# A one-level Strassen scheme for the down projection of a decoder block on one Trainium2 core

## The chip, the cores and the metric

The kernel runs on one core of one Trainium2 chip. The metric is the device time of one execution in microseconds. Before the change the median of three runs is 1080.75 us (1080.3 to 1080.9). The engines are TensorE (PE, with its weight loads as PEld), VectorE (DVE), ScalarE (ACT), GpSimd (POOL) and SyncE (SP), and sixteen DMA engines move data.

## The reference

One decoder layer on 512 tokens of width 1024. What matters here is the second half, the gated MLP with a short causal convolution, and the layer norm behind it:

```python
def channel_mixer(h, w_up, ffn_dw_w, ffn_dw_b, w_down):
    u = jnp.einsum("bsd,df->bsf", h, w_up)
    u = causal_depthwise_conv(u, ffn_dw_w, ffn_dw_b)
    val, gate = jnp.split(u, 2, axis=-1)
    return jnp.einsum("bsf,fd->bsd", val * jax.nn.silu(gate), w_down)

# in reference():
f = channel_mixer(h, w_up[l], ffn_dw_w[l], ffn_dw_b[l], w_down[l])
x = layer_norm(DEEPNORM_ALPHA * x + gate2 * f, ln2_g[l], ln2_b[l])
```

`w_down` is 2816 x 1024 in float32. The down projection is so a product of (512 x 2816) with (2816 x 1024).

## The kernel before

Float32 matmuls are made of three terms: an operand is split into a high part `h` (a ScalarE copy to the matmul's type) and a low part `l` (a VectorE subtraction), and a product is the sum of h.h, l.h and h.l. So each 128-row block of each product costs three matmuls, and each weight a split on ScalarE and VectorE.

The weights come through one stream (class `Stream`): SyncE loads an entry of up to 1 MB into one of two `stage` buffers, L126; a piece of up to 1024 columns is then split into one of three `wh` and `wl` buffers, L140 and L141. `get` returns the next piece and splits up to two ahead.

The stages, with their place in the profiled execution: the start-up (to about 50 us) normalizes the input, computes modulation vectors (`dot`, L326, on VectorE, from weights `wa` that `load_first` asks SyncE for, three buffers) and does the first projections; the head stage (to about 450 us) goes through eight heads, with a 31-tap convolution on VectorE (L460) beside TensorE's projections; gates, output projections and the first layer norm follow (to about 715 us), the up projection (to about 946 us), and the down projection with the last layer norm.

The work is written as a program in which each engine has one queue in order. The tile framework puts each engine's instructions in an order of its own, from their dependences, free buffers and priorities (`later(n)` lowers a priority by n places), and adds the semaphores.

GpSimd does little: it clears the padding of the convolution inputs (L454) and raises variances to the power -1/2 (`rstd_of`, L228), for the norm of the input, once for each head, and for each layer norm.

The up projection makes two units of 24 matmuls for each of the 22 blocks of the hidden layer. `up_pair(j, ...)` applies the convolution and the gate and splits the result into `acts[j]`, an `(ah, al)` pair of 128 features x 512 tokens.

The down projection (L1044 to L1084) runs in two passes. The first goes over the 22 blocks k and over four token tiles s of 128; its result is 512 columns (`pd0`) and then 256 columns (`pd1`). The last 256 columns have weights of their own (`wdq`), loaded and split during the first pass (`load_wq`, `split_wq`). The second pass does them token tile by token tile, so that the sum and the layer norm of one tile (`resid`, L865 and L866; `norm_rows`, L871 and L872) run beside the matmuls of the next. The stationary operand is a slice of `acts`, the moving one the weights.

Of the kernel before, what the change touches and what calls it, by code (L numbers as in the profile page):

```python
# [9 lines left out]
F32 = mybir.dt.float32  # L10
F32R = mybir.dt.float32r
# [13 lines left out]
CK = 31  # L25
DFF = 2816
NF = DFF // P
FK = 3
EPS = 1e-5
ALPHA = 2.0 ** 0.25  # L30
# [71 lines left out]
class Stream:  # L102
# [18 lines left out]
    def load(self, i):  # L121
        if i < len(self.entries) and i not in self.stage:
            ap, widths, pre = self.entries[i]
            w = sum(widths)
            t = self.pool.tile([P, 2048], F32, tag="stage", bufs=2, name=f"stage{i}")
            self.nc.sync.dma_start(t[:, :w], ap)  # L126
            self.stage[i] = t

    def prefetch(self, n):
# [43 lines left out]
def block_kernel(ctx: ExitStack, tc: tile.TileContext, a, out):  # L173
# [43 lines left out]
    def big(name):  # L217
        return [base.tile([P, ND, S], F32R, tag=f"big{i}", bufs=1, name=f"{name}{i}") for i in range(2)]
# [50 lines left out]
    for j in range(NF // 2):  # L269
        entries.append((a["wdn"][j], [768, 768]))  # L270
    st = Stream(nc, base, entries, 2)


# [327 lines left out]
    def drive(g):  # L601
        if g is not None:
            next(g, None)

    g = None
# [353 lines left out]
    drive(tr_[3])  # L959


    acts = []

    def up_out(p_, t):
        u = lg("u")
        act(u, p_, AF.Identity, bias=vc("fb", t), scale=vc("fw", t * FK + 2))
        stt(u[:, 1:], p_[:, :S - 1], vc("fw", t * FK + 1), u[:, 1:], ALU.mult, ALU.add)
        stt(u[:, 2:], p_[:, :S - 2], vc("fw", t * FK), u[:, 2:], ALU.mult, ALU.add)
        return u

    def up_pair(j, pv, pgt):
        r = [up_out(pv, j), up_out(pgt, NF + j)]
        act(r[1], r[1], AF.Silu)
        tt(r[0], r[0], r[1], ALU.mult)
        al = lg if j < 9 else xg if j < 13 else pg
        x, y = al("ah", F32R), al("al", F32R)
        split_to(x, y, r[0])
        acts.append((x, y))

    def half_unit(p_, w, half):  # L980
        c = slice(half * 256, (half + 1) * 256)
# [34 lines left out]
        up_pair(j, pv, pgt)  # L1016


    wqh, wql = big("wq")
    wq = []  # L1020

    NQ = NF // 2
    WQD = 3
    for c in range(NQ):
        if c < 8:
            x, y = wqh[:, c], wql[:, c]
        else:
            x, y = pg("wqh", F32R), pg("wql", F32R)
        wq.append((x, y))

    wqs = {}

    def load_wq(c):

        wqs[c] = lg("wqs")
        nc.sync.dma_start(wqs[c], a["wdq"][:, c * 512:(c + 1) * 512])

    def split_wq(c):
        t = wqs.pop(c)
        split_to(wq[c][0], wq[c][1], t)  # L1040

    pd0 = [ps("d0") for _ in range(NS)]
    pd1 = [ps("d1", (P, 2, DV)) for _ in range(2)]
    for k in range(NF):  # L1044
        wh, wl = st.get()
        if 1 <= k <= NQ:
            load_wq(k - 1)
        if WQD < k <= WQD + NQ:
            split_wq(k - WQD - 1)
        for s in range(NS):  # L1050
            sl = slice(s * P, (s + 1) * P)
            x, y = acts[k]
            f, l = (k == 0), (k == NF - 1)
            d1 = pd1[s // 2][:, s % 2]
            f1 = f and s % 2 == 0
            mm(pd0[s], x[:, sl], wh[:, 0:512], start=f, stop=False)  # L1056
            mm(pd0[s], y[:, sl], wh[:, 0:512], start=False, stop=False)  # L1057
            mm(pd0[s], x[:, sl], wl[:, 0:512], start=False, stop=l)  # L1058
            mm(d1, x[:, sl], wh[:, 512:768], start=f1, stop=False, skip_group_check=True)  # L1059
            mm(d1, y[:, sl], wh[:, 512:768], start=False, stop=False, skip_group_check=True)  # L1060
            mm(d1, x[:, sl], wl[:, 512:768], start=False, stop=l, skip_group_check=True)  # L1061
    lnr = []
    for name, tag in (("ln2_g", "wh"), ("ln2_b", "wl")):
        t = base.tile([P, D], F32, tag=tag, bufs=3, name=name)
        nc.sync.dma_start(t, a[name].broadcast_to([P, D]))
        lnr.append([t[:, 0:512], t[:, 512:1024]])
    ln2g, ln2b = lnr

    for s in range(NS):
        resid(xs[s][0], pd0[s], rows["gate2"][0])  # L1070
        resid(xs[s][1], pd1[s // 2][:, s % 2], rows["gate2"][1], slice(0, 256))
    for s in range(NS):
        sl = slice(s * P, (s + 1) * P)
        p_ = ps("d2", (P, DV))
        for k in range(NF):
            x, y = acts[k]
            wh, wl = wq[k // 2]
            w = slice((k % 2) * DV, (k % 2 + 1) * DV)
            mm(p_, x[:, sl], wh[:, w], start=(k == 0), stop=False)  # L1079
            mm(p_, y[:, sl], wh[:, w], start=False, stop=False)  # L1080
            mm(p_, x[:, sl], wl[:, w], start=False, stop=(k == NF - 1))  # L1081
        resid(xs[s][1], p_, rows["gate2"][1], slice(256, 512))
        norm_rows(xs[s], [xs[s][0], xs[s][1][:, :256], xs[s][1][:, 256:]], ln2g, ln2b,
                  lambda j: nc.sync.dma_start(out[s * P:(s + 1) * P, j * 512:(j + 1) * 512], xs[s][j]))  # L1084


# [95 lines left out]
```

## Time and profile before

| what | value |
|---|---|
| median of 3 runs | 1080.75 us |
| the profiled execution, its own time | 1080.97 us |
| its span, first to last instruction | 1079.2 us |
| TensorE busy | 1054.4 us, 98% |
| VectorE busy | 785.8 us, 73% |
| ScalarE busy | 456.6 us, 42% |
| GpSimd busy | 26.3 us, 2% |
| moved by DMA | 131.54 MB, mean 122 GB/s |
| granted TensorE clock, mean | 0.999 |

A busy TensorE is not TensorE at its peak, since matmuls are pipelined; what a stage costs is read from the starts of its matmuls and from the gaps between them. DMA-issuing instructions are not counted as busy.

### The profile page before, as it was taken

Reading aid. Unit: us, or ns where it says so; the run is one execution under the profiler, and the core shown is the slowest. Engines: PE = TensorE matmul, PEld = TensorE weight load, DVE = VectorE, ACT = ScalarE, POOL = GpSimd, SP = SyncE. Lnnn points to the kernel's source line nnn. Section 1 sums busy time; section 2 is a strip of 40 time slices with the busy share of each in tenths; the row PEclk is TensorE's granted clock in tenths of the full one; section 3 lists DMA queues with packets and bytes.
Section 4 is the critical chain, followed back from the end, with each engine's and each line's share of the span. In section 5 each row is a group of like instructions: output and inputs, shape, how many; then the busy total and the mean of one; then the engine's idle time right before and its main releaser. Section 6 shows DMA issues by size and latency. Waiting matters only on the chain. (4 is left out here: it accounts for less than half of the span.)

```text
span 1079.2 us, 14096 instructions
## 1 busy us (share of the span) xinstructions
PE 1054.4 (98%) x5648; PEld 906.9 (84%) x5648; DVE 785.8 (73%) x1252; ACT 456.6 (42%) x655; POOL 26.3 (2%) x41
## 2 busy tenths in 40 slices
PE   4999999999999999999999999999999999999997
PEld 2788898989898988887888889898888888888896
DVE  7989999979797979498984446957666565652264
ACT  5753544353444344551363333465444444442100
POOL 1000000000000000000000000110000000000001
PEclk9999999999999999999999999999999999999999
DMA  8822313222322222378642256022222323153112
GB/s 314 309 87 87 122 50 120 86 90 84 121 81 92 84 78 79 137 250 293 241 176 94 104 189 215 1 79 78 105 90 85 111 83 113 62 192 112 65 40 79
DMA packets 29316, 131.54 MB, mean 122 GB/s; under 512 B 3393, under 2 KB 5697, under 8 KB 19522
## 3 DMA queue, kind: packets, MB, share of 16 engines
q1 hardware_dynamic: 29250, 130.64, 34.1%
q8 instruction: 44, 0.72, 0.3%
q14 instruction: 22, 0.18, 0.1%
HBM read 128.53 MB, written 2.10 MB: 121 GB/s over the span
## 5 line engine op out<-in xcount | busy, mean ns | idle before, releaser
L141 DVE TENSOR_TENSOR wl<-stage,wh 128x1024 fp32r<-128x1024 f32 (+1 forms) x163 | 193.2, 1185 | 151.0 <-ACT wh L140 53.2
L140 ACT ACTIVATE wh<-stage 128x1024 fp32r<-128x1024 f32 (+1 forms) x163 | 168.0, 1030 | 291.7 <-PE up L442 58.0
L460 DVE SCALAR_TENSOR_TENSOR conv<-ci,vec,conv 128x512 f32<-128x512 f32 x240 | 178.8, 745 | 2.3
L441 PE MATMUL up<-h,wh 128*128 128x512 f32 x304 | 118.3, 389 | 0.0
L442 PE MATMUL up<-h,wh 128*128 128x512 f32 x304 | 118.3, 389 | 0.0
L444 PE MATMUL up<-h,wl 128*128 128x512 f32 x304 | 75.1, 389 | 0.0
L490 PE MATMUL v<-wl,h 128*128 128x256 f32 x256 | 72.5, 283 | 0.4 <-DVE wl L141 0.4
L489 PE MATMUL v<-wh,h 128*128 128x256 f32 x256 | 72.4, 283 | 0.0
L488 PE MATMUL v<-wh,h 128*128 128x256 f32 x256 | 72.4, 283 | 0.0
L441 PEld LDWEIGHTS up<-h,wh 128*128 128x128 f32 x304 | 57.1, 188 | 11.8
L444 PEld LDWEIGHTS up<-h,wl 128*128 128x128 f32 x304 | 57.1, 188 | 11.8
L442 PEld LDWEIGHTS up<-h,wh 128*128 128x128 f32 x304 | 57.1, 188 | 11.8
L782 PE MATMUL yb<-rh,wh 128*128 128x512 f32 x128 | 51.0, 398 | 0.0
L783 PE MATMUL yb<-rl,wh 128*128 128x512 f32 x128 | 50.5, 395 | 0.0
L784 PE MATMUL yb<-rh,wl 128*128 128x512 f32 x128 | 50.5, 395 | 0.0
L441 PE MATMUL gate<-h,wh 128*128 128x512 f32 x128 | 50.2, 392 | 0.0
L442 PE MATMUL gate<-h,wh 128*128 128x512 f32 x128 | 50.0, 390 | 0.0
L490 PEld LDWEIGHTS v<-wl,h 128*128 128x128 f32 x256 | 49.1, 192 | 0.6 <-DVE wl L141 0.6
L488 PEld LDWEIGHTS v<-wh,h 128*128 128x128 f32 x256 | 49.1, 192 | 0.0
L489 PEld LDWEIGHTS v<-wh,h 128*128 128x128 f32 x256 | 49.1, 192 | 0.0
L442 PE MATMUL g<-h,wh 128*128 128x512 f32 x112 | 43.7, 390 | 0.0
L441 PE MATMUL g<-h,wh 128*128 128x512 f32 x112 | 43.6, 389 | 0.0
(295 smaller groups left out, 2499.9 us busy)
## 6 DMA issues: line engine op xcount, KB each, us to landing
stage<-in_wstep SPq DMA_DIRECT2D x29, 1024.0 KB, 4.8
stage<-in_wup SPq DMA_DIRECT2D x22, 1024.0 KB, 4.8
wb<-in_wada SPq DMA_DIRECT2D x32, 512.0 KB, 5.3
stage<-in_wdn SPq DMA_DIRECT2D x11, 768.0 KB, 4.3
stage<-in_wret SPq DMA_DIRECT2D x8, 1024.0 KB, 5.9
stage<-in_wga SPq DMA_DIRECT2D x8, 1024.0 KB, 4.9
wa<-in_wada SPq DMA_DIRECT2D x14, 512.0 KB, 6.4
stage<-in_wgb SPq DMA_DIRECT2D x4, 1024.0 KB, 4.8
```

The source lines that it names most:

```text
L140: nc.scalar.activation(wh[:, :w], src, AF.Copy)
L141: nc.vector.tensor_tensor(wl[:, :w], src, wh[:, :w].bitcast(F32), ALU.subtract)
L441: mm(dst, wh[:, k * P:(k + 1) * P], hs[k][0], start=(k == 0), stop=False)
L442: mm(dst, wh[:, k * P:(k + 1) * P], hs[k][1], start=False, stop=False)
L444: mm(dst, wl[:, k * P:(k + 1) * P], hs[k][0], start=False, stop=(k == n - 1))
L460: stt(o, ci[:, t:t + S], vc("cw", i * CK + t), o, ALU.mult, ALU.add)
L488: mm(d, h_h[:, k, sl], wh[:, r], start=(k == 0), stop=False)
L489: mm(d, h_l[:, k, sl], wh[:, r], start=False, stop=False)
L490: mm(d, h_h[:, k, sl], wl[:, r], start=False, stop=(k == ND - 1))
L782: mm(p_, wh[:, w], rs_[k][0], start=(k == 0), stop=False)
L783: mm(p_, wh[:, w], rs_[k][1], start=False, stop=False)
L784: mm(p_, wl[:, w], rs_[k][0], start=False, stop=(k == 15))
```

## The change

The down projection is cut into halves in three ways: tokens 0 to 255 and 256 to 511; the 22 hidden blocks into even and odd ones (11 pairs); the output columns into 0 to 511 and 512 to 1023. Of the four weight blocks B11, B12, B21, B22 (each 1408 x 512) four sums are made: T1 = B11 + B12, T3 = B12 + B22, T2 = T1 + B22, T4 = T2 + B21. They lie in DRAM. Each is copied there by DMAs that GpSimd issues and then added to by DMAs with `accum_op`; 36 issues, of which the program names five at the top of each head's loop.

Seven products of 256 tokens x 1408 x 512 take the place of the two passes. They come in the order B11, T1, B21, T2, T3, B22, T4, each with 11 blocks x 2 token tiles x 3 terms. The activations stay unsplit in `F` (`u` of `up_pair`); their sums and differences are made on VectorE in place, and `split_op` splits the 256-token operand of a product, in `up_pair` for the first two products and for the others (`make`) during the product before. The weight stream has 21 entries of up to 1 MB here where it had 11 of 768 KB; entries of B12 and B22 are two DMAs with rows of 1 KB, as half of their columns lie in `wdq`. The results are gathered in `ca`, `c5`, `cb_`, `cc_` and in `xs`, with part of that work under `later(40)`. Token tiles 0 and 1 are finished after the sixth product, 2 and 3 after the seventh, whose last five blocks are done token tile by token tile. The rows of the last norm are loaded early, into the space of `h2`.

```diff
+    dram = ctx.enter_context(tc.tile_pool(name="dram", bufs=1, space=bass.MemoryType.DRAM))
+    for name in ("T1", "T2", "T3", "T4"):
+        wd[name] = dram.tile([P, NK, 512], F32, tag=name, name=name)
+    PIECES = ((0, 4), (4, 8), (8, 11))
...
+    for name in ("B11", "T1", "B21", "T2", "T3", "B22", "T4"):
+        for x, y in PIECES:
+            w = (y - x) * 512
+            entries.append((wblock(name, x, y), [1024, w - 1024]))
...
+    def sum_steps():
+        for dst, first, add in (("T1", "B11", "B12"), ("T3", "B12", "B22"), ("T2", "T1", "B22"), ("T4", "T2", "B21")):
+            for x, y in PIECES:
+                for f, src in wblock(first, x, y):
+                    nc.gpsimd.dma_start(wd[dst][:, x:y, f], src)
+                    yield
+            for x, y in PIECES:
+                for f, src in wblock(add, x, y):
+                    nc.gpsimd.dma_start(wd[dst][:, x:y, f], src, accum_op=ALU.add)
+                    yield
...
     for i in range(NH):
+        for _ in range(5):
+            drive(sums)
...
+        F.append(u)
+        if j % 2:
+            i = j // 2
+            x, y = F[2 * i], F[2 * i + 1]
+            ops1.append(split_op(i, x[:, 0:256]))
+            e = pg("e1", F32, (P, 256))
+            tt(e, x[:, 256:], y[:, 256:], ALU.subtract)
+            ops5.append(split_op(i, e))
+            tt(x[:, 256:], x[:, 256:], x[:, 0:256], ALU.subtract)
+            tt(x[:, 0:256], x[:, 0:256], e, ALU.subtract)
...
+    for n, R in enumerate((R1, R2, R1, R2, R3, R2, R3)):
+        new = n in (0, 1, 4)
+        ops = operands.pop(n)
+        made = []
+        for q in range(6 if n < 6 else 3):
+            w = st.get()
+            for kk in range(2 if q < 5 else 1):
+                k = 2 * q + kk
+                for t in range(2):
+                    sub_mm(R, ops[k], w, kk, t, new and k == 0, k == NK - 1)
+                if 1 <= n < 6:
+                    made.append(make(n + 1, k))
...
+        elif n == 4:
+            for t in range(2):
+                tt(cc_[t], R3[t], cb_[t], ALU.add)
+            with later(40):
+                for t in range(2):
+                    tt(c5[t], c5[t], cb_[t], ALU.subtract)
+                    tt(c5[t], c5[t], g2[0], ALU.mult)
+                    stt(xs[2 + t][0], xs[2 + t][0], ALPHA, c5[t], ALU.mult, ALU.add)
+                    tt(cc_[t], cc_[t], g2[1], ALU.mult)
+                    stt(xs[2 + t][1], xs[2 + t][1], ALPHA, cc_[t], ALU.mult, ALU.add)
+        elif n == 5:
+            for t in range(2):
+                tt(ca[t], R2[t], ca[t], ALU.subtract)
+            with later(40):
+                for t in range(2):
+                    tt(ca[t], ca[t], g2[1], ALU.mult)
+                    stt(xs[t][1], xs[t][1], ALPHA, ca[t], ALU.mult, ALU.add)
+                    finish(t)
         else:
+            ws_ = [st.get(ahead=2 - q) for q in range(3)]
+            for t in range(2):
+                for q in range(3, 6):
+                    for kk in range(2 if q < 5 else 1):
+                        k = 2 * q + kk
+                        sub_mm(R, ops[k], ws_[q - 3], kk, t, False, k == NK - 1)
+                tt(R[t], R[t], g2[0], ALU.mult)
+                tt(xs[2 + t][0], xs[2 + t][0], R[t], ALU.subtract)
+                finish(2 + t)
```

`sub_mm` issues the three matmuls of one block and token tile, 512 columns each; `make(n, k)` is one `split_op` on 256 columns, and for n = 2 a subtraction on 256 columns more; `finish(s)` is `norm_rows` and the two stores.

## Rows read from the trace of the kernel before

**Rows 1.** Busy time of each engine over the span, instructions.
```profile
PE 1054.4 (98%) x5648; PEld 906.9 (84%) x5648; DVE 785.8 (73%) x1252; ACT 456.6 (42%) x655; POOL 26.3 (2%) x41
```
**Rows 2.** Windows: stretch, length, busy of each engine, PE clock, DMA share, GB/s.
```profile
15.00:20.00 5.00, 0.95 (x2) 0.36 (x2) 4.05 (x12) 4.73 (x8) 1.75 (x2) 1.00 1.04 415
...
25.00:50.00 25.00, 24.00 (x117) 19.37 (x116) 24.41 (x49) 16.79 (x29) 0.00 (x0) 1.00 0.92 340
...
100.00:200.00 100.00, 100.00 (x580) 88.28 (x579) 97.89 (x158) 44.90 (x64) 2.81 (x5) 1.00 0.29 102
...
946.50:1039.50 93.00, 93.00 (x529) 81.06 (x529) 32.35 (x41) 24.21 (x33) 0.00 (x0) 1.00 0.33 110
1039.50:1071.20 31.70, 31.70 (x267) 31.54 (x265) 21.10 (x46) 0.00 (x0) 2.69 (x3) 1.00 0.14 51
```
**Rows 3.** Order of time on PE: start, duration, line, tiles; triples, stage's ends.
```profile
479.74 0.39 PE L782 MATMUL yb<-rh,wh 128*128 128x512 f32 x1
...
481.83 0.40 PE L782 MATMUL yb<-rh,wh 128*128 128x512 f32 x1
...
946.78 0.40 PE L1056 MATMUL d<-wh,ah 128*128 128x512 f32 x1
...
1069.77 0.28 PE L1080 MATMUL d<-wqh,al 128*128 128x256 f32 x1
...
1070.97 0.28 PE L1081 MATMUL d<-wql,ah 128*128 128x256 f32 x1
```
**Rows 4.** Order of time on DVE at the end of the kernel.
```profile
1071.29 0.43 DVE L865 TENSOR_TENSOR d<-d,grow 128x256 f32<-128x256 f32 x1 [3.39 <-PE d L1081]
...
1073.01 1.40 DVE L871 SCALAR_TENSOR_TENSOR xr<-xr,mv,ln_g 128x512 f32<-128x512 f32 x2
1074.33 1.41 DVE L872 SCALAR_TENSOR_TENSOR xr<-xr,rstd,ln_b 128x512 f32<-128x512 f32 x2
```
**Rows 5.** Groups by form on DVE and ACT: busy us, mean ns, idle before.
```profile
L141 DVE TENSOR_TENSOR wl<-stage,wh 128x1024 fp32r<-128x1024 f32 x141 | 172.1, 1221 | 102.2 <-PE up L444 41.8 <-PE gate L444 25.6 <-PE cg L444 14.6
L249 DVE TENSOR_TENSOR Rl<-R,Rh 128x256 fp32r<-128x256 f32 x8 | 3.3, 417 | 0.0
L865 DVE TENSOR_TENSOR d<-d,grow 128x512 f32<-128x512 f32 x4 | 2.8, 692 | 7.4 <-PE d L1058 7.4
...
L140 ACT ACTIVATE wh<-stage 128x1024 fp32r<-128x1024 f32 x141 | 149.4, 1060 | 240.7 <-PE up L442 51.9 <-PE v L489 41.7 <-PE yb L783 35.8
L248 ACT ACTIVATE Rh<-R 128x256 fp32r<-128x256 f32 x8 | 3.1, 384 | 0.2
```
**Rows 6.** Order of time on POOL: padding, a root of the input's norm, head 0's root.
```profile
0.73 0.23 POOL L454 MEMSET ci<- 128x30 f32 x3 [0.29 <-POOLq L1170]
...
10.06 0.57 POOL L228 TENSOR_TENSOR rstd<-ve,cst 128x1 f32<-128x1 f32 x1 [4.09 <-DVE ve L239]
...
115.28 1.42 POOL L228 TENSOR_TENSOR rstd<-hve,cst 128x4 f32<-128x4 f32 x1 [8.12 <-DVE hve L583]
```
**Rows 7.** Order of time: a VectorE operation that reads a mask, and SP's next load.
```profile
89.45 0.55 DVE L534 TENSOR_TENSOR scf<-sc,dm 128x384 f32<-128x384 f32 x1
...
90.03 0.33 SPq L504 DMA_DIRECT2D dm<-in_dmask  x1
```
**Rows 8.** DMA queue (packets, MB, share of sixteen engines); issues (KB, us to landing).
```profile
q1 hardware_dynamic: 29250, 130.64, 34.1%
...
stage<-in_wup SPq DMA_DIRECT2D x22, 1024.0 KB, 4.8
```
**Rows 9.** Modulation weights: a load's issue, its use on DVE, landing times of all.
```profile
33.80 0.33 SPq L314 DMA_DIRECT2D wa<-in_wada  x1
...
43.30 1.22 DVE L326 SCALAR_TENSOR_TENSOR junk<-wa,cb 128x1024 f32<-128x1024 f32 x1
...
DMA to landing us min/median/max: 3.8/6.5/10.3
```
**Rows 10.** Order of time on PE: the transposes of head 0's normed values.
```profile
122.02 1.03 PE L594 MATMUL rT<-cst,rn 128*128 128x128 f32 x8
```

More of the change, by code (lines that the diff above doesn't have):

```diff
@@ L27 @@
 NF = DFF // P
+NK = NF // 2
 FK = 3
@@ L125, in load @@
             t = self.pool.tile([P, 2048], F32, tag="stage", bufs=2, name=f"stage{i}")
-            self.nc.sync.dma_start(t[:, :w], ap)
+            if isinstance(ap, list):
+                v = t[:, :w].rearrange("p (j f) -> p j f", f=512)
+                for f, x in ap:
+                    self.nc.sync.dma_start(v[:, :, f], x)
+            else:
+                self.nc.sync.dma_start(t[:, :w], ap)
             self.stage[i] = t
@@ L268, in block_kernel, with wblock @@
         entries.append((a["wup"][j], [1024, 1024]))
-    for j in range(NF // 2):
-        entries.append((a["wdn"][j], [768, 768]))
+    dram = ctx.enter_context(tc.tile_pool(name="dram", bufs=1, space=bass.MemoryType.DRAM))
+    wd = {}
+    for name in ("T1", "T2", "T3", "T4"):
+        wd[name] = dram.tile([P, NK, 512], F32, tag=name, name=name)
+    PIECES = ((0, 4), (4, 8), (8, 11))
+    def wblock(name, x, y):
+        if name in wd:
+            return [(slice(0, 512), wd[name][:, x:y])]
+        r, c = int(name[1]) - 1, int(name[2]) - 1
+        n = a["wdn"][x:y].rearrange("j p (t f) -> p j t f", t=2)[:, :, r]
+        if c == 0:
+            return [(slice(0, 512), n[:, :, 0:512])]
+        q = a["wdq"].rearrange("p (j t f) -> p j t f", t=2, f=256)[:, x:y, r]
+        return [(slice(0, 256), n[:, :, 512:768]), (slice(256, 512), q)]
+    for name in ("B11", "T1", "B21", "T2", "T3", "B22", "T4"):
+        for x, y in PIECES:
+            w = (y - x) * 512
+            entries.append((wblock(name, x, y), [1024, w - 1024]))
     st = Stream(nc, base, entries, 2)
@@ L603, in drive @@
             next(g, None)
+    def sum_steps():
[8 more added lines that the diff above has]
+                    yield
+    sums = sum_steps()
     g = None
     for i in range(NH):
+        for _ in range(5):
+            drive(sums)
         if i == 0:
@@ L969, in up_out, with op_page, split_op @@
         return u
-    def up_pair(j, pv, pgt):
[L972 to L978, printed above, removed]
+    F = []
+    ops1, ops5 = [], []
+    def op_page(i):
+        return (pg if i < 8 else xg)("op", F32R, (P, 2, 256))
+    def split_op(i, src, neg=False):
+        o = op_page(i)
+        if neg:
+            act(o[:, 0], src, AF.Copy, scale=-1.0)
+            stt(o[:, 1], src, -1.0, o[:, 0].bitcast(F32), ALU.mult, ALU.subtract)
+        else:
+            split_to(o[:, 0], o[:, 1], src)
+        return o
+    def up_pair(j, pv, pgt):
+        u = up_out(pv, j, lg if j < 21 else pg)
+        r = up_out(pgt, NF + j, pg)
+        act(r, r, AF.Silu)
+        tt(u, u, r, ALU.mult)
+        F.append(u)
[8 more added lines that the diff above has]
+            tt(x[:, 0:256], x[:, 0:256], e, ALU.subtract)
     def half_unit(p_, w, half):
@@ L1042, in block_kernel @@
[L1042 to L1084, printed above, removed]
+    dt0 = base.tile([P, ND, S], F32, tag="big0", bufs=1, name="dtmp")
@@ new lines, in block_kernel, with finish @@
+    dt1 = base.tile([P, ND, S], F32, tag="big1", bufs=1, name="drow")
+    ca, c5, cb_, cc_ = [[dt0[:, 2 * n + t] for t in range(2)] for n in range(4)]
+    lnr = []
+    for n, name in enumerate(("ln2_g", "ln2_b")):
+        r = [dt1[:, 2 * n + h] for h in range(2)]
+        for h in range(2):
+            nc.sync.dma_start(r[h], a[name][:, h * 512:(h + 1) * 512].broadcast_to([P, 512]))
+        lnr.append(r)
+    ln2g, ln2b = lnr
+    g2 = rows["gate2"]
+    def finish(s):
+        norm_rows(xs[s], [xs[s][1], xs[s][0]], ln2g, ln2b,
+                  lambda j: nc.sync.dma_start(out[s * P:(s + 1) * P, j * 512:(j + 1) * 512], xs[s][j]))
@@ new lines, in block_kernel, with make, sub_mm @@
+    R1, R2, R3 = [[ps(f"d{n}") for _ in range(2)] for n in range(3)]
+    def make(n, i):
+        x, y = F[2 * i], F[2 * i + 1]
+        if n == 2:
+            o = split_op(i, y[:, 0:256])
+            tt(y[:, 0:256], y[:, 0:256], x[:, 0:256], ALU.subtract)
+            return o
+        src = {3: x[:, 0:256], 4: x[:, 256:], 5: y[:, 0:256], 6: y[:, 256:]}[n]
+        return split_op(i, src, neg=(n == 6))
+    def sub_mm(R, o, w, kk, t, start, stop):
+        wh, wl = w
+        c = slice(kk * 512, (kk + 1) * 512)
+        sl = slice(t * P, (t + 1) * P)
+        mm(R[t], o[:, 0, sl], wh[:, c], start=start, stop=False, skip_group_check=True)
+        mm(R[t], o[:, 1, sl], wh[:, c], start=False, stop=False, skip_group_check=True)
+        mm(R[t], o[:, 0, sl], wl[:, c], start=False, stop=stop, skip_group_check=True)
@@ new lines, in block_kernel @@
+    operands = {0: ops1, 1: ops5}
+    for n, R in enumerate((R1, R2, R1, R2, R3, R2, R3)):
[10 more added lines that the diff above has]
+                    made.append(make(n + 1, k))
+        if made:
+            operands[n + 1] = made
+        if n == 0:
+            for t in range(2):
+                act(ca[t], R1[t], AF.Copy)
+        elif n == 1:
+            for t in range(2):
+                act(c5[t], R2[t], AF.Copy)
+        elif n == 2:
+            for t in range(2):
+                resid(xs[t][0], R1[t], g2[0])
+        elif n == 3:
+            for t in range(2):
+                tt(cb_[t], R2[t], ca[t], ALU.subtract)
+        elif n == 4:
+            for t in range(2):
+                tt(cc_[t], R3[t], cb_[t], ALU.add)
+            with later(40):
+                for t in range(2):
+                    tt(c5[t], c5[t], cb_[t], ALU.subtract)
[4 more added lines that the diff above has]
+        elif n == 5:
+            for t in range(2):
+                tt(ca[t], R2[t], ca[t], ALU.subtract)
+            with later(40):
+                for t in range(2):
+                    tt(ca[t], ca[t], g2[1], ALU.mult)
+                    stt(xs[t][1], xs[t][1], ALPHA, ca[t], ALU.mult, ALU.add)
+                    finish(t)
+        else:
+            ws_ = [st.get(ahead=2 - q) for q in range(3)]
+            for t in range(2):
+                for q in range(3, 6):
[5 more added lines that the diff above has]
+                finish(2 + t)
```

21 lines of the change are left out of this document (2 added, 19 removed).

## The prediction

> **What bounds the kernel now.** I read the busy time by engine first: TensorE is busy for 98% of the span and VectorE for 73% [rows 1]. A busy TensorE need not be the bound, so next come the windows by stage: in the down projection, 946.5 to 1071.2 us, TensorE has no gap at all, while VectorE works 53 of 125 us and the queues carry 110 and 51 GB/s [rows 2]. So this stage is paid in matmuls. The third view is the order of time on TensorE, for the price of one, from start to start: in triples of 512 columns, each with weights of its own, nine steps take 2.09 us, 0.2322 a matmul; at 256 columns ten steps take 1.20, 0.12 a matmul [rows 3]. The stage begins at 946.78 and its last matmul starts at 1070.97 [rows 3]. Last I read the end: VectorE takes the last sum at 1071.29 and its last pair of operations runs from 1074.33 to 1075.74 [rows 4]; the span ends at 1079.2, so the tail behind TensorE's end (1071.2) is 8.0 us, 3.5 of it behind VectorE's end.
>
> **TensorE.** Removed: 22 x 4 x 3 = 264 matmuls of 512 columns and 2 x 264 of 256, 124.4 us by the ends above, with 0.2 for the last one. Added: 7 products x 11 blocks x 2 token tiles x 3 terms = 462 of 512 columns, in triples like those of [rows 3]: 462 x 0.2322 = 107.3 us, 15.33 us a product. Saved: 17.1 us, taken as 17.0. (In the up projection, where two matmuls in turn share their weights, the step is shorter; the new triples don't share, so I don't use it.)
>
> **VectorE in the stage.** The durations in [rows 5] overlap by some 0.08 us: a pair of operations that lasts 1.40 us is followed after 1.32, 0.66 for each [rows 4]. So a split of 1024 columns costs 1.14, one operation on 512 columns 0.61, on 256 columns 0.34, a scaled one 0.66. A product needs 5 x 1.14 + 0.61 = 6.3 us for its weights and 11 x 0.34 = 3.7 for the operands of the next; the second product has 11 more of 0.34. The first five need 6 to 14 us each of their 15.33: covered. ScalarE needs 5 x 1.06 + 0.6 + 11 x 0.38 = 10 us a product: covered too.
>
> The sixth and seventh are not. From the sixth's start VectorE has: weights that are not yet split, 7 x 1.14 + 2 x 0.61 = 9.2; operands of the seventh, 3.7; the fifth's sums, 2 x 0.61 = 1.2, and its ten late operations, 6.1; the sixth's sums, 1.2, its four late operations, 2.4, and two layer norms of 4.1 (two statistics, two small operations, four of 0.66), 8.2. That is 32.0 us. Up to where the last row block's matmuls begin there are 2 x 15.33 - 3.5 = 27.2 us (15 matmuls, 3.5 us, are the last token tile's). A backlog of 4.8 us is left, or about 1 if operands are made earlier, where VectorE has room. Then come two more pairs of sums and two layer norms, 10.6 us, and the 3.5 us that follow now too (GpSimd's power runs beside the two operations of a norm that don't need it). The end lies at -3.5 + (1 to 4.8) + 10.6 + 3.5 = 11.6 to 15.4 us behind TensorE, 10.6 with no backlog; now it is 8.0. I charge 5 us, bounds 3 and 9 (the upper one if late sums get in front of splits). What makes TensorE shorter is thus partly given back: the cover of the last norms was the 31.7 us of 256-column matmuls, and it is gone.
>
> **The loads of the stage.** 21 loads, 20.2 MB in 107 us: 188 GB/s against 110 now. Each of the two staging buffers must turn round in 11.2 us; a load of 1 MB lands 4.8 us after its issue [rows 8], and the queues have moved 415 GB/s [rows 2]. Rows of 1 KB in two of the blocks may slow it; up to about 7 us to landing nothing waits. Cost 0, upper bound 3 us. In the up projection VectorE's work grows by 5 x 0.34 - 2 x 0.61 = 0.5 us for two blocks: nothing. What leaves the queues there (the 11 loads of the last quarter) is worth nothing either.
>
> **The sums in DRAM.** Four blocks are made: each is a copy of 1408 x 512 x 4 B = 2.88 MB and an accumulating DMA over it, 36 issues of GpSimd, 11.5 MB copied and 11.5 MB added. No row shows a DMA from DRAM to DRAM, nor one that adds. The nearest price is that of the loads: 130.64 MB took 34.1% of sixteen engines over 1079.2 us [rows 8], so 355 GB/s at full share, or 8.1 us for a block; I bound the copy by one and two such times (it writes to DRAM what it reads there), the adding one by two and three. All eight come to 100 to 160 us of the queues. In the head stage their share is 0.29, in 100 to 200 us [rows 2], and the sums are wanted only after 946: there is room.
>
> What matters is when they start. The code issues five for each head, but a queue holds what its instructions' producers allow: GpSimd's clearing of the padding of heads 0, 1 and 2 stands at 0.73 us, ahead of work that the program names earlier [rows 6], and the mask for head 2 is asked for at 90.03, when its buffer falls free at the end of a VectorE operation, more than one head early [rows 7]. The copies into the first and the third sum (nine DMAs, 5.8 MB) wait for nothing, so I take them to start at about 1 us, into the start-up, where the queues are 0.92 to 1.04 busy [rows 2]. Nobody waits for those loads, though: a piece of the modulation weights is asked for at 33.80, lands after 6.5 us in the median, and is used at 43.30 [rows 9]: 3 us of slack, and VectorE, busy for 24.4 of 25 us, is what the start waits for. A load that takes half as long again costs nothing; one that takes twice as long costs a few us at each of the eight steps. I charge 5 us, bounds 0 and 16: at the load's price the copies take 5.8 MB / 355 GB/s = 16 us of the queues, and the slack covers part of it.
>
> The Trainium skill (DMA: Bandwidth & Descriptors, Latency and other measured facts) gives 207 GB/s per direction for copies between HBM tensors. By that figure, an estimate, the nine copies would hold the queues for 28 us and the charge would grow by 12 us and the sum below end near 1086; no row here shows it.
>
> **Sum.** Against the profiled execution's own 1080.97 us (span 1079.2; the median of the runs is 0.2 lower, which I neglect): 1081.0 - 17.0 + 5 + 0 + 5 = **1074**. Its own bounds: 1081.0 - 17.0 + 3 = 1067, and 1081.0 - 17.0 + 7 + 8 = 1079.
>
> **Rivals.**
> *The start-up pays for the copies.* If a copied byte costs two loaded ones, or the adding DMAs follow while the start-up still runs, 16 to 28 us are lost before the first head: 1081 - 12 + 16 = 1085, up to 1097. Slower than before from the point where the loss passes 12 us. For it: the queues have no share free at 10 to 25 us; against it: the slack of [rows 9].
>
> *GpSimd's queue stands.* An adding DMA must wait until the copy beneath it has landed, and it waits in GpSimd's queue; behind it stand the reciprocal roots that GpSimd makes, at 10.06 for the input's norm and at 115.28 for head 0 [rows 6]. TensorE takes head 0's normed values at 122.02 [rows 10], 7 us later. If the sums in the queue ahead of that root run past 122, TensorE stands for the rest: with all 100 to 160 us of sums ahead of it, 20 to 50 us are lost, 1095 to 1120. Against it: the roots are short and come ready early, and by program order only ten of the 36 issues belong ahead of head 0's root.
> The Trainium skill (DMA: Bandwidth & Descriptors, Rules for kernel authors) asks for this wait: an accumulate must wait for the semaphore of an earlier DMA on the same bytes. By that rule the queue does stand, if only for a landing each time; that no run here shows.
>
> *VectorE bounds the last products.* If the backlog delays weight splits, TensorE stands in the sixth and seventh product and the tail has its upper price: 1081 - 17 + 9 + 5 + 3 (the loads' bound) = 1081, no change.
>
> That the work doesn't shrink is excluded by the count of matmuls.
>
> **How the numbers follow.** Forecast 0.52, start-up 0.20, queue 0.15, VectorE 0.13. A difference under 0.2% (2.2 us) can't be told from none here. Faster by more: nearly all of the forecast and a fifth of the VectorE case, 0.52. Within: 0.05 x 0.52, most of the VectorE case and a tenth of the start-up case, 0.14. Slower: 0.34. The range must take in the forecast, the VectorE case, the start-up case and the lower part of the queue case: 1066 to 1100 leaves out some 0.14.
>
> **What would show it.** TensorE: 462 matmuls behind the up projection, from first to last start 107 us; more means that it waits there, and the releaser tells whether for a split or a load. Tail: 11 to 16 us from TensorE's last matmul to the end, VectorE without idle time in it. Start-up: the first head's matmuls begin within 5 us of now; VectorE's waits for loads of modulation weights show the first rival. Head stage: TensorE's gaps ahead of the transposes of normed values, GpSimd's power late against its operand, show the second. The forecast is wrong if the head stage loses more than 12 us, or if the down stage isn't bound by matmuls.

## The result and the profile after

The changed kernel takes 1092.01 us in the median of four runs (1090.28 to 1093.29), the kernel before beside it 1080.61 us: a ratio of 1.0105 (95% interval 1.0087 to 1.0122). The forecast was 1074 us and the sign was wrong: the change costs 11.4 us. The profiled execution took 1093.29 us, with a span of 1091.2.

The stage that the change is about did what was forecast. First the windows of the profile after (stretch, length, busy time and instructions of PE, PEld, DVE, ACT and POOL, granted clock, DMA share, GB/s): the head stage, the down projection, and the tail.

```profile
100.00:200.00 100.00, 97.63 (x552) 85.38 (x551) 92.22 (x151) 43.05 (x61) 15.29 (x16) 0.97 0.71 196
969.06:1076.50 107.44, 107.44 (x464) 86.91 (x462) 91.01 (x153) 59.90 (x101) 1.62 (x2) 1.00 0.53 176
1076.50:1091.20 14.70, 0.15 (x1) 0.00 (x0) 11.17 (x21) 0.00 (x0) 2.07 (x3) 0.58 0.29 107
```

Beside [rows 2]: the down projection now holds 107.4 us of TensorE without a gap, where 93.0 and 31.7 stood; behind it lie 14.7 us instead of 8.0. The stage and its tail went from 132.4 to 122.1 us. Its start is what moved: the first matmul of the down projection stands at 969.1 us, and [rows 3] had it at 946.78, so 22.3 us were lost ahead of it. 22.3 - 10.3 is the 12.0 us by which the span grew. The group of the first of the three terms (shortest, median and longest ns, then first and last start in us):

```profile
L1111 PE MATMUL d<-wh,op x154: 390/393/404, 969.1 to 1075.8; 128*128 128x512 f32 x154
```

Where the 22.3 us went is seen on TensorE and GpSimd early in the kernel. The order of time on TensorE (start, duration; in brackets the idle time ahead and what ended it), the first transpose of the input, before:

```profile
11.72 0.48 PE L408 MATMUL xT<-cst,x 128*128 128x128 f32 x1 [4.50 <-ACT x L342]
```

and after, with the transposes of head 0's normed values, which answer to [rows 10]:

```profile
22.47 0.48 PE L433 MATMUL xT<-cst,x 128*128 128x128 f32 x1 [15.14 <-ACT x L367]
...
140.44 2.69 PE L619 MATMUL rT<-cst,rn 128*128 128x128 f32 x8 [2.37 <-ACT rn L613]
```

10.75 us are lost before the first transpose, 16.0 by the time VectorE has head 0's last variance (131.00, shown below, against 115.04), and 22.8 when GpSimd makes head 0's root (138.05 against 115.28), which is all of the 22.3. The transposes come only 18.4 us late (140.44 against 122.02), since TensorE had by then done the work that stood ahead of them before. Behind the root nothing more is lost: head 1's root follows it after 51.50 us, and before after 51.36. The variance and head 1's root before, and head 1's root after:

```profile
115.04 0.15 DVE L583 TENSOR_TENSOR hve<-hmv,cst 128x2 f32<-128x2 f32 x1
...
166.64 1.01 POOL L228 TENSOR_TENSOR rstd<-hve,cst 128x4 f32<-128x4 f32 x1 [22.27 <-DVE hve L583]
```

```profile
189.55 1.01 POOL L234 TENSOR_TENSOR rstd<-hve,cst 128x4 f32<-128x4 f32 x1 [22.28 <-DVE hve L608]
```

GpSimd's order of time after, beside [rows 6]:

```profile
1.28 1.73 POOL L634 DMA_DIRECT2D T<-in_wdn  x2 [0.83 <-POOLq L1255]
...
15.86 0.57 POOL L234 TENSOR_TENSOR rstd<-ve,cst 128x1 f32<-128x1 f32 x1 [4.18 <-DVE ve L245]
16.39 0.83 POOL L634 DMA_DIRECT2D T<-in_wdn  x1
...
30.52 3.58 POOL L634 DMA_DIRECT2D T<-in_wdn  x1
...
59.80 0.14 POOL L479 MEMSET ci<- 128x30 f32 x1
...
118.24 0.58 POOL L634 DMA_DIRECT2D T<-T  x1 [5.37 <-DMA T<-in_wdq]
...
138.05 1.53 POOL L234 TENSOR_TENSOR rstd<-hve,cst 128x4 f32<-128x4 f32 x1
```

Two copies of 1 MB leave at 1.28 us, ahead of all of GpSimd's other work but four constants; the third copy of the first sum leaves at 16.39, and those of the third sum begin at 30.52. All 36 DMAs of the sums stand ahead of head 0's root, which comes at 138.05 us instead of 115.28 and has no wait of its own: it was merely behind the last of them. VectorE had its operand ready at 131.0 us, and then waited:

```profile
131.00 0.15 DVE L608 TENSOR_TENSOR hve<-hmv,cst 128x2 f32<-128x2 f32 x1
...
139.62 0.16 DVE L611 SCALAR_TENSOR_TENSOR hnb<-hmv,rstd 128x4 f32<-128x4 f32 x1 [7.20 <-POOL rstd L234]
```

The DMA issues (KB each, median us from issue to landing) show what the input met. Over the span before, the input's tiles land after

```profile
x<-in_x SPq DMA_DIRECT2D x8, 256.0 KB, 5.0
```

and after the change, with the new queue's packets, MB and share of sixteen engines,

```profile
q0 software_dynamic: 12608, 23.07, 9.2%
...
wa<-in_wada SPq DMA_DIRECT2D x14, 512.0 KB, 11.3
T<-in_wdn POOLq DMA_DIRECT2D x4, 1024.0 KB, 10.8
...
T<-T POOLq DMA_DIRECT2D x4, 1024.0 KB, 18.5
...
x<-in_x SPq DMA_DIRECT2D x8, 256.0 KB, 9.0
```

The modulation weights (`wa`) take 11.3 us, where [rows 9] has 6.5.

### The profile page after: what moved, and what is told of

It reads as the page before. It is cut to its first block, busy times and chain, and to the rows that moved or that the text cites. A ratio compares the mean times of both kernels' runs of the same rounds, so it can differ in the third digit from the quotient of the medians.

```text
span 1091.2 us, 13688 instructions
## 1 busy us (share of the span) xinstructions
PE 1043.2 (96%) x5318; PEld 884.7 (81%) x5318; DVE 836.3 (77%) x1360; ACT 489.1 (45%) x723; POOL 63.4 (6%) x77
## 3 DMA queue, kind: packets, MB, share of 16 engines
q0 software_dynamic: 12608, 23.07, 9.2%
## 5 line engine op out<-in xcount | busy, mean ns | idle before, releaser
L147 DVE TENSOR_TENSOR wl<-stage,wh 128x1024 fp32r<-128x1024 f32 x183 | 219.5, 1200 | 133.7 <-PE up L469 57.4
L146 ACT ACTIVATE wh<-stage 128x1024 fp32r<-128x1024 f32 x183 | 190.9, 1043 | 283.5 <-PE up L467 56.1
L469 PEld LDWEIGHTS up<-h,wl 128*128 128x128 f32 x304 | 57.1, 188 | 11.8
L466 PEld LDWEIGHTS up<-h,wh 128*128 128x128 f32 x304 | 57.1, 188 | 11.8
L467 PEld LDWEIGHTS up<-h,wh 128*128 128x128 f32 x304 | 57.1, 188 | 11.8
L1111 PE MATMUL d<-wh,op 128*128 128x512 f32 x154 | 60.8, 395 | 0.0
L1112 PE MATMUL d<-wh,op 128*128 128x512 f32 x154 | 60.8, 395 | 0.0
L1113 PE MATMUL d<-wl,op 128*128 128x512 f32 x154 | 60.8, 394 | 0.0
## 6 DMA issues: line engine op xcount, KB each, us to landing
wa<-in_wada SPq DMA_DIRECT2D x14, 512.0 KB, 11.3
```

What stands on the lines that cost most here:

```text
L146: nc.scalar.activation(wh[:, :w], src, AF.Copy)
L147: nc.vector.tensor_tensor(wl[:, :w], src, wh[:, :w].bitcast(F32), ALU.subtract)
L466: mm(dst, wh[:, k * P:(k + 1) * P], hs[k][0], start=(k == 0), stop=False)
L467: mm(dst, wh[:, k * P:(k + 1) * P], hs[k][1], start=False, stop=False)
L469: mm(dst, wl[:, k * P:(k + 1) * P], hs[k][0], start=False, stop=(k == n - 1))
L1111: mm(R[t], o[:, 0, sl], wh[:, c], start=start, stop=False, skip_group_check=True)
```

## The experiments

Three reasons are to be told apart: the copies that run beside the loads of the input (start-up), the sums' traffic beside the loads from about 17 to 80 us (traffic), and the roots that stand behind the sums on GpSimd (queue). The cause could also lie in the new products. In the diffs `roots` is the list of GpSimd's root instructions, and `issue_after(r)` keeps what it encloses behind `r` on GpSimd, without a wait.

**The change without its sums** (the diff; its weights for the products with sums are other weights, so its output is not the layer's), and **the kernel before with `sum_steps` and its five `drive(sums)` for each head**, whose result nobody reads:

```diff
-            entries.append((wblock(name, x, y), [1024, w - 1024]))
+            if name[0] == "T":
+                entries.append((a["wup"][x][:, :w], [1024, w - 1024]))
+            else:
+                entries.append((wblock(name, x, y), [1024, w - 1024]))
...
-        for _ in range(5):
-            drive(sums)
```

> The changed kernel without its 36 DMAs of GpSimd; the weights of the four products with sums are read from the up projection's weights instead, in rows of the same 8 KB, so the output is not the layer's. Theory A (all of the loss is where the sums run: the down stage began 22.3 us late, and from its first matmul to the end it takes 122.1 us against 132.4): 1070.6 us, the down stage begins at 947 and lasts 122. Rival (the seven products or their weight rows cost more elsewhere, for example in the up projection or in the pages): above 1075, with the down stage beginning later than 949.

> The kernel before, with the 36 sum DMAs of the change at the same place and nothing reading the sums. Theory A: the sums alone cost what the start of the down stage lost, 22 us: 1103 us, three steps (first transpose 11 us late, then 6, then 6 at head 0's root). Rival (part of the loss comes from the new products' code): clearly less than 1098.

Without the sums: 1071.01 us (1070.11 to 1072.0), 0.9906 of before (0.9891 to 0.9921). The kernel before with unused sums: 1101.18 us in one run, 20 above before. So the products are worth about 10 us and the sums cost about 20, whichever kernel they are put in.

**All sums behind roots of later heads**, six DMAs for each of heads 2 to 7:

```diff
-        for _ in range(5):
-            drive(sums)
+        if i >= 2:
+            with tc.issue_after(roots[-1]):
+                for _ in range(6):
+                    drive(sums)
```

> The changed kernel with the same 36 DMAs, in batches of six at heads 2 to 7, each queued behind the last root that GpSimd has made by then (an order of issue only), so none runs before about 115 us and none stands ahead of head 0's root. Theory A (the sums cost only where the start-up's loads or a root stand behind them): 1071 us, down stage begins within 2 us of 947. Rival (23 MB cost time wherever they run, by loads of weights that come late or by GpSimd's queue in each head): 1080 or more, with gaps on TensorE in the head stage.

1071.03 us (1069.99 to 1071.68), 0.9903 of before (0.9886 to 0.9919): as good as without sums, and faster than both kernels. The same bytes now move in the head stage. Its windows, of which the first answers to the head stage's in [rows 2]:

```profile
100.00:200.00 100.00, 99.77 (x575) 88.03 (x576) 97.90 (x158) 44.90 (x64) 15.16 (x17) 1.00 0.60 175
200.00:300.00 100.00, 100.00 (x579) 88.27 (x579) 87.93 (x143) 44.81 (x64) 13.80 (x16) 1.00 0.55 162
300.00:400.00 100.00, 100.00 (x579) 88.27 (x579) 87.83 (x142) 44.44 (x64) 15.19 (x14) 1.00 0.67 176
```

The DMA share doubles from 0.29 to 0.60 and TensorE keeps working: the sums are free here. This is the reference for the next runs.

**The start-up alone.** The last version with the three copies of the first sum let go as early as they like (in e7: one piece of 1 MB):

```diff
+        if i == 0:
+            for _ in range(3):      # e7: drive(sums) once
+                drive(sums)
```

> As the kernel with late sums, but the three copies into the first sum (2.88 MB) are left free, so that they go first, at about 1 us. Theory A1 (the first of the three losses, 10.7 us at the first transpose, is made by these copies alone, which slow the input's loads): 1071 + 10 = 1081 us, first transpose at 21 to 22.5 us. Rival A2 (it needs the later DMAs too, or GpSimd's queue with its waits): under 1076, first transpose before 16.

> As the kernel with late sums, with one copy of 1 MB left free, so that it goes first. With three free copies (two of them, 2 MB, went ahead of the input's loads) the loss was 9.8 us. If the price goes by bytes from the first one on: 1071 + 5 = 1076 us, first transpose at 17. If the first MB finds idle queues (share 0.31 in the first 5 us): under 1073, first transpose at 12 to 13.5.

2.88 MB of copies, of which 2 MB leave ahead of the input's loads, cost 10.4 us (1081.39, one run): the first transpose stands at 22.81 us. A single 1 MB copy costs 3.2 us (1074.21, one run), in between the two expectations; the first transpose at 16.98 us is 4.9 later than at 12.04, of which 1.7 come back. The trace of the run with one copy shows the way: ScalarE waits 8.9 us for a tile of the input.

```profile
ACT tr L392 <- DMA x<-in_x: 8.9, 1, 8.9
```

**The queue.** All sums behind the four roots of the input's norm, but ahead of head 0's as in the change; and, the other way round, the last 15 DMAs behind head 0's root, the rest as in the change:

```diff
 # behind the input's norm
         for _ in range(5):
-            drive(sums)
+            with tc.issue_after(roots[3]):
+                drive(sums)
 # half behind head 0's root: 21 at head 0, then three for each of heads 2 to 7
+        if i == 0:
+            for _ in range(21):
+                drive(sums)
+        if i >= 2:
+            with tc.issue_after(roots[-1]):
+                for _ in range(3):
+                    drive(sums)
```

> The changed kernel with all 36 DMAs queued behind the four roots of the input's norm (an order of issue only), so none starts before about 17 us; all 36 still stand ahead of head 0's root. In the changed kernel the sums ran from 1.3 to 138 us. Theory Q (GpSimd's queue is a loss of its own: the root waits for what is left of the sums): the first loss of 10 us is gone, but the sums end 10 to 15 us later against a root that is due 10 us earlier, so the third loss grows from 6 to 15 or 30: 1087 to 1103 us, root at 135 or later. Theory C (only the queues' load in the start-up costs): 1071 + 6 to 12 = 1077 to 1083 us, root before 128.

> The changed kernel with the last 15 of the 36 DMAs (the second and fourth sum) queued behind head 0's root, the first 21 as free as before. Theory Q: the third loss (6.2 us) alone is gone, the first two stay: 1092 - 6 = 1086 us, head 0's transposes without a gap ahead of them. Theory C: the transposes come where they did, 1090 or more.

Neither helped: 1093.69 us (ratio 1.0115, 1.0086 to 1.0144) and 1091.58 us (one run). By their expectations the first speaks for the queue and the second against it; either run alone would have misled, and the traces explain the pair. With the sums behind the input's norm the first transpose is back at 11.75 us and head 0's variances are there at 120.75, but the root still stands behind the last sum (order of time on VectorE and GpSimd; then that run's waits from 85 to 145 us, with total, times and longest):

```profile
120.75 0.17 DVE L610 TENSOR_TENSOR hve<-hmv,cst 128x2 f32<-128x2 f32 x1
...
139.74 1.53 POOL L236 TENSOR_TENSOR rstd<-hve,cst 128x4 f32<-128x4 f32 x1
...
POOL T L640 <- DMA T<-T: 26.4, 4, 22.6
DVE hnb L613 <- POOL rstd L236: 19.1, 1, 19.1
```

VectorE waited 19.1 us instead of 7.2. What the input's loads no longer lost, the queue took. With 15 of the 36 DMAs behind the root, the root no longer waited for a sum, but another victim came up in GpSimd's queue, the padding of the convolutions (then a wait of that run):

```profile
82.24 0.73 POOL L481 MEMSET ci<- 128x30 f32 x3
...
136.22 1.42 POOL L236 TENSOR_TENSOR rstd<-hve,cst 128x4 f32<-128x4 f32 x1 [9.62 <-DVE hve L610]
...
ACT conv L485 <- POOL ci L481: 3.1, 1, 3.1
```

Three pads, 0.73 us of the kernel before [rows 6], now stand at 82.24 behind an adding DMA; ScalarE's convolution waits 3.1 us for one, VectorE's operations come in another order, and the variances are ready only at 136.0 us.

**Both at once.** To take that victim out, VectorE writes the pads, and the first 21 DMAs go as early as in the change, or behind the input's norm:

```diff
-        nc.gpsimd.memset(ci[:, :CK - 1], 0.0)
+        nc.vector.memset(ci[:, :CK - 1], 0.0)
 # the second version, beside it: behind the input's norm
         if i == 0:
-            for _ in range(21):
-                drive(sums)
+            with tc.issue_after(roots[3]):
+                for _ in range(21):
+                    drive(sums)
```

> The change with the first 21 DMAs of the sums as they were, the last 15 behind head 0's root, and the convolutions' zero pads (128x30) written by VectorE instead of GpSimd. In the run that moved the 15 DMAs alone, three pads stood behind the adding DMAs (82.24 us) and ScalarE's convolution waited 3.1 us for one; head 0's variances were there at 136.0 us instead of the change's 131.0. Theory of two covers (the late input loads and GpSimd's queue lie side by side, each enough for most of the loss): with the pads off the queue the variances are there at 131 to 133 us, the root comes right behind them, and the run takes 1086 to 1088 us, still 15 us above the version with all sums late, because of the input's loads and the stage loads. Theory that the DMA traffic of the sums slows everything by itself: no change from 1091.6 us.

> The same, with the first 21 DMAs of the sums behind the four roots of the input norm as well: neither the input's loads nor head 0's root meets the sums, only the loads from 17 us on do. Theory of two covers: the variances of head 0 are there near 121 us, as in the run with all sums behind the input norm (120.75 us), the root follows at once instead of at 139.7 us, and the run takes 1076 to 1078 us, 5 to 7 us above all sums late: the price of the traffic between 20 and 80 us. Theory that the traffic alone makes most of the loss: 1085 us or more.

1083.28 us (one run), 3 us better than expected: the pads had cost 8.3 us there (1091.58 - 1083.28), more than the 3.1 us of the wait that I had seen; where the rest of it goes was not followed. And 1077.18 us (one run), as expected. Head 0's root in the two traces, with nothing but its operand ahead of it:

```profile
127.88 1.42 POOL L236 TENSOR_TENSOR rstd<-hve,cst 128x4 f32<-128x4 f32 x1 [45.16 <-DVE hve L610]
```

```profile
121.85 1.43 POOL L236 TENSOR_TENSOR rstd<-hve,cst 128x4 f32<-128x4 f32 x1 [38.09 <-DVE hve L610]
```

All of them in one table (first transpose of the input, head 0's last variance, head 0's root, and the time of the same, profiled execution; us):

| kernel | transpose | variance | root | run | run - root |
|---|---|---|---|---|---|
| all sums late | 12.0 | 115.9 | 116.1 | 1071.6 | 955.5 |
| one piece early | 17.0 | 118.7 | 119.0 | 1074.2 | 955.2 |
| half behind the input's norm, half behind root 0 | 11.6 | 121.6 | 121.9 | 1077.2 | 955.3 |
| first copies early | 22.8 | 125.7 | 125.9 | 1081.4 | 955.5 |
| half as in the change, half behind root 0, pads on VectorE | 22.2 | 127.6 | 127.9 | 1083.3 | 955.4 |
| the same, pads on GpSimd | 22.5 | 136.0 | 136.2 | 1091.6 | 955.4 |
| the change | 22.5 | 131.0 | 138.1 | 1093.3 | 955.2 |
| all behind the input's norm | 11.8 | 120.8 | 139.7 | 1093.9 | 954.2 |

The last column is the same within 1.3 us, and within 0.3 but for the last row: the loss is complete when head 0's root is made, and nothing behind it costs or gives back much. The start-up alone costs 10.4 us; the traffic alone 6.2, with waits of ScalarE for the weights of the first projections (`w`, 8.3 us in all, none with late sums); the two together 12.3, both with the pads on VectorE; and the queue alone 16.5 beyond the traffic (1093.7 - 1077.2, the last 15 DMAs ahead of the root or behind it). These are covers, not terms: 10.4 + 6.2 + 16.5 would be 33, and the change loses 21.0 against the version with late sums. Whatever the start-up loses is taken off the wait for the queue. One difference stays open: the change has its variance 3.4 us later than the version with the last 15 DMAs late and the pads on VectorE (131.0 and 127.6), and no run tells which of the two does it.

**The tail.** The last version with late sums, without the norms of the first two token tiles:

```diff
     def finish(s):
+        if s < 2:                   # tiles 0 and 1 are stored without their norm
+            ...
+            return
```

> The kernel with late sums, with the last layer norm of token tiles 0 and 1 left out (they are stored as they are, so half of the output is not normalized): 8.2 us less for VectorE while the seventh product runs. Theory V (VectorE's backlog makes the tail longer, 15 us behind TensorE's end): the tail falls to 10.6 us, 1071 - 4 = 1067 us. Rival (the last tile's own chain sets the tail, backlog or not): 1070 or more, tail 14 to 15.

1065.77 us (one run), 5.3 less than with late sums: two norms, 8.2 us of VectorE by the prediction's prices, and VectorE then waits 2.4 us for the last products. The tail is 10.5 us long there, where 10.6 was expected without a backlog. So the tail is VectorE's backlog. Two ways to shorten it, without leaving anything out:

```diff
 # norms of tiles 0 to 2 shared
...
+            stt(x[j], x[j], nmu, ln2g[j], ALU.subtract, ALU.mult)
+            act(x[j], x[j], AF.Copy, scale=rs)
+            nc.gpsimd.tensor_tensor(x[j], x[j], ln2b[j], ALU.add)
...
 # joining sums on GpSimd (six operations)
-                    tt(c5[t], c5[t], cb_[t], ALU.subtract)
+                    nc.gpsimd.tensor_tensor(c5[t], c5[t], cb_[t], ALU.subtract)
...
```

> All sums late, and the last norms of row tiles 0 to 2 shared: mean and gain on VectorE, the factor of the root on ScalarE, the row that is added on GpSimd. VectorE loses three pairs of 128x512 operations (1.41 us a pair). Theory that the tail is VectorE's backlog: 2.5 to 4 us faster than all sums late (1071.0 us), so 1067 to 1068.5 us. Theory that the last tile's own chain sets the end, whatever stands in front of it: within 0.7 us of 1071.0 us. If GpSimd's additions or ScalarE's factors end last, it is between the two or above.

> All sums late, and six of the element-wise operations that join the products (c5 minus cb, c5 times its gate, cc times its gate, two 128x512 tiles each) on GpSimd instead of VectorE. They are 4 us of VectorE's work in the last 20 us (0.68 us each). Theory of the backlog: 2 to 4 us faster than 1071.0 us where GpSimd's results are there before VectorE comes to them. If GpSimd takes long over a 128x512 operation or the two engines slow each other, no gain or a loss: 1071 to 1075 us.

Shared norms: 1069.74 us (1069.24 to 1070.84), 0.9898 of before (0.9884 to 0.9913), the lowest time of a complete version, but 1.3 us from the version with late sums instead of 2.5 to 4. That is too little to be told from it here, where the intervals overlap. The sums on GpSimd: 1072.55 us (0.9923, 0.9907 to 0.994), not faster. Both met the same thing. VectorE's scaled operations of a norm (group, count, busy us, mean ns), with late sums and with shared norms:

```profile
L915 DVE SCALAR_TENSOR_TENSOR xr<-xr,mv,drow 128x512 f32<-128x512 f32 x8 | 5.7, 744 | 0.0
```

```profile
L1100 DVE SCALAR_TENSOR_TENSOR xr<-xr,mv,drow 128x512 f32<-128x512 f32 x6 | 5.8, 988 | 0.0
...
L915 DVE SCALAR_TENSOR_TENSOR xr<-xr,mv,drow 128x512 f32<-128x512 f32 x2 | 2.4, 1244 | 0.0
```

Eight such operations went from 5.7 to 8.2 us: 2.5 of the 4.2 us (three pairs of 1.41) that had been taken off VectorE came back as slower work beside GpSimd's additions. With the joining sums on GpSimd it is the weight splits and the sums behind the fifth product that are hit (order of time on VectorE, then on GpSimd):

```profile
1009.38 1.72 DVE L147 TENSOR_TENSOR wl<-stage,wh 128x1024 fp32r<-128x1024 f32 x1
...
1012.28 1.77 DVE L1153 SCALAR_TENSOR_TENSOR xr<-xr,dtmp 128x512 f32<-128x512 f32 x1 [1.18 <-POOL dtmp L1152]
1015.23 0.69 DVE L1153 SCALAR_TENSOR_TENSOR xr<-xr,dtmp 128x512 f32<-128x512 f32 x1 [1.19 <-POOL dtmp L1152]
...
1007.87 2.14 POOL L1151 TENSOR_TENSOR dtmp<-dtmp 128x512 f32<-128x512 f32 x1 [294.80 <-DVE dtmp L1145]
1010.10 2.15 POOL L1152 TENSOR_TENSOR dtmp<-dtmp,grow 128x512 f32<-128x512 f32 x1
1012.21 1.29 POOL L1151 TENSOR_TENSOR dtmp<-dtmp 128x512 f32<-128x512 f32 x1
```

A split takes 1.72 us instead of the usual 1.22. VectorE's scaled operation of L1153 takes 1.77 us where GpSimd's subtraction had begun just ahead of it (1012.21), and 0.69 us at 1015.23, beside none. GpSimd's subtraction takes 1.29 us there, and 2.14 at 1007.87, where a split of VectorE had begun ahead of it. And VectorE waits for GpSimd's result, 1.18 us at the line shown.

## Why the prediction was wrong, step by step

*TensorE, right.* 462 matmuls, forecast 107.3 us: from the first start at 969.06 to the last at 1076.27 are 107.2 us, with no gap. *VectorE in the last products, right:* TensorE did not stand there, so that rival did not come. *The loads of the stage, right for TensorE:* those of 1 MB land after 4.8 to 5.2 us and TensorE never waits. ScalarE waited for three of them in the stage, 6.6 us in all, and the last (4.19 us from 1062.52) stands on the chain that ended last.

*The tail, right in mechanism and within its bounds.* Forecast 11.6 to 15.4 us behind TensorE, measured 14.7, near the upper end, with VectorE continuously at work till 1087.7; I had charged 5 us against before and it is 6.7. The backlog is not only work that exceeds the time, as the sum had it: between 1052 and 1061 us VectorE still stood for 5.2 us, waiting for ScalarE's splits and for the sixth product's results. (By its own prices the late operations come to 6.3 and 2.5 us, not 6.1 and 2.4.) In the version with late sums 15.0 us. There the forecast's terms can be put in as measured: 1081.0 - 17.2 + 7.0 (tail) + 0.8 (start of the stage, 947.6 against 946.78) = 1071.6, and that execution took 1071.64. The forecast without its charge for the sums is 1069; of the 2.6 us more, 2.0 are the tail.

*The sums in DRAM, the step that failed.* Charged 5 us, bounds 0 to 16; they cost 21.0. How long they hold the queues was right: I said 100 to 160 us, and the new queue's 9.2% of sixteen engines over 1091.2 us is 100 us. That copies would start at about 1 us was right for two of the nine, 2 MB; the others followed from 16.39 and from 30.52 us on. Two readings were wrong:

1. "Nobody waits for those loads." I took the modulation weights, with 3 us of slack, for all loads of the start-up. For them the reading held: they landed after 11.3 us, and VectorE waited for them 1.4 us in all; but ScalarE waited 8.4 us for `w`. The copies met the loads that stand first in the queue, the input's tiles, and TensorE has nothing else to do before these are normed: 4.50 us idle ahead of the first transpose before, 15.14 after. [rows 6] had shown the input's first root at 10.06 us, right behind a wait; I read the row for GpSimd and not for what it waits on. The run with the first copies alone early puts this at 10.4 us.
2. "By program order only ten of the 36 issues belong ahead of head 0's root." All 36 stood ahead of it. I had argued from [rows 6] and [rows 7] that an instruction is placed as early as its producers allow, and applied that to the copies but not to the adding DMAs, whose only producers are the copies. With it the queue's case follows from the numbers that I had: 100 to 160 us of sums from 1.3 us on, with waits for landings between them, against a root due at 115.28. VectorE stood for it, 7.2 us in the change and 19.1 without the loss at the start; TensorE, which I had taken to stand, did so for 2.4 us in the change. The last adding DMA was let go at 137 us. That case was priced at 1095 to 1120 for 0.15; the start-up at 1085 to 1097 for 0.20. The result, 1092, lies in the start-up's bounds, but both came, each hiding the other: the first copies alone make 1081, the queue without the start-up 1094.

The Trainium skill (DMA: Bandwidth & Descriptors, Rules for kernel authors) asks that an accumulate wait for the semaphore of an earlier DMA on the same bytes; the trace agrees, and the wait is long: up to 22.6 us in one of the runs. The Trainium skill's figure for copies between HBM tensors (DMA: Bandwidth & Descriptors, Latency and other measured facts), 207 GB/s, which the page gives for rows 512 KiB apart, led to an estimate near 1086 us; the new queue's 23.07 MB, copied and added together, in 100 us of sixteen engines are 230 GB/s, so that figure was nearer than the loads' 355. No run prices a copy by itself, and the loss did not come from this price.

*The chances.* The time lay inside the range, at 1092 of 1066 to 1100, but 0.52 of the chance was on the wrong side. The point at which the change turns slower, a loss of 12 us ahead of the stage, was near: the stage and its tail gave 10.3.

## What to carry to other kernels

An instruction without producers can go far ahead of the place where the program names it, as the pads and the first copies did here, and everything on that engine that comes later in the order waits through its waits: before a slow DMA is put on an engine that also makes a small value for others, list that engine's whole queue in order, not the program's. Put background transfers behind an instruction of the stage that has the room; here the order alone was worth 21 us. When two causes lie side by side, undoing one can show nothing: undo both, and then put each back alone.

## What the runs showed of the hardware

Behind the wait for head 0's root the granted clock of TensorE fell. Windows after the change:

```profile
138.00:140.00 2.00, 0.07 (x1) 0.00 (x0) 0.38 (x2) 0.18 (x1) 1.59 (x3) 1.00 1.12 203
140.00:142.00 2.00, 1.56 (x4) 0.74 (x5) 2.00 (x3) 2.00 (x5) 0.00 (x0) 0.55 1.13 208
142.00:144.00 2.00, 2.00 (x8) 1.80 (x8) 2.00 (x4) 2.00 (x4) 0.00 (x0) 0.50 1.13 209
144.00:146.00 2.00, 2.00 (x6) 1.51 (x6) 2.00 (x4) 0.46 (x1) 0.00 (x0) 0.50 1.10 190
146.00:148.00 2.00, 2.00 (x8) 1.63 (x7) 2.00 (x3) 0.00 (x0) 0.00 (x0) 0.74 1.07 185
148.00:150.00 2.00, 2.00 (x10) 1.63 (x10) 1.97 (x4) 1.60 (x2) 0.00 (x0) 1.00 1.12 276
```

TensorE had stood for the 2.4 us ahead; then it worked at 0.50, 1.2 GHz, until past 146 us, with matmuls of 512 columns 0.43 us apart (144.21, 144.63, 145.06) instead of 0.23. It cost the run next to nothing here: VectorE was busy throughout from 140 to 148 us, and head 1's root came 51.50 us behind head 0's, 0.14 more than before.

The input's loads of 256 KB landed after 9.0 us instead of 5.0 beside copies of 1 MB from GpSimd's queue, though they stand first among the large loads on SyncE's own; and SyncE took 8.17 us instead of 3.75 to issue the eight of them. The Trainium skill (DMA: Bandwidth & Descriptors, Queues, rings and completion order) says that each DMA engine takes turns between its queues packet by packet; the trace agrees in that both queues were served at once.

VectorE and GpSimd slow each other on operations with two inputs (VectorE's split from 1.22 to 1.72 us and its scaled operation from 0.69 to 1.77, GpSimd's subtraction from 1.29 to 2.14). The Trainium skill (SBUF — State Buffer, SBUF: two separate sides) has the two engines lock a shared port for a whole instruction when a VectorE operation reads two tensors from SBUF beside a GpSimd operation that reads there too. The trace agrees: where GpSimd began 0.07 us ahead it took its short 1.29 us, and VectorE's operation ended 0.55 us behind it, most of the 0.69 us that it takes alone. The delay of the split, 0.5 us, is less than the other engine's whole operation, which a lock taken in the middle of it also gives.
